# A two-layer transformer kernel: other PSUM banks for three small products, a re-ordered first stretch, and three sums moved behind more products

## The chip, the cores and the metric

The kernel runs on one core of a Trainium2 chip. A core has TensorE (PE; its weight loads are shown as PEld), VectorE (DVE), ScalarE (ACT) and GpSimd (POOL, unused here); SyncE (SP) issues the DMAs, which 16 DMA engines carry out. Each engine works through its own list of instructions in order. The metric is the device time of one execution in microseconds (us).

## The reference, cut to what matters

Two layers over 256 tokens of width 1024. Each is a token mixer with two attentions and a convolutional feed-forward part; every part is modulated by a vector from `c`, and followed by a layer norm.

```python
for l in range(2):
    mod = silu(c) @ w_ada[l] + b_ada[l]            # 6 x 1024
    sh1, sc1, g1, sh2, sc2, g2 = split(mod, 6)
    h = x * (1 + sc1) + sh1
    y = token_mixer(h, ...)
    x = layer_norm(ALPHA * x + g1 * y, ...)
    h = x * (1 + sc2) + sh2
    x = layer_norm(ALPHA * x + g2 * conv_ffn(h, ...), ...)

def token_mixer(h, positions, rel_bias, w_in, ...):
    qa, ka, va, iq, ik, iw, cq, ckv, kr, ga, gb = split(h @ w_in)
    # a: index scores choose 64 of 256 keys per query; softmax(qa.ka + rel_bias[bucket(distance)]) va
    # b: q = rms_norm(cq) @ w_uq, (k, v) = rms_norm(ckv) @ w_ukv, rope on a part; softmax(q.k) v
    merged = sigmoid(ga) * (ya @ w_branch_a) + sigmoid(gb) * (yb @ w_branch_b)
    return merged @ w_out
```

`rel_bias` depends on the position distance through 32 buckets; the kernel builds that table of biases itself, once, from 64 thresholds.

## The kernel before, in words

**Layout.** Activations stand with the 1024 channels as 8 chunks of 128 partitions and the 256 tokens along the free side. Weights come from HBM in one long `stream` of units of up to 128x2048 numbers (1 MB), through four `raw` buffers; a unit's DMA waits until the unit four before it is used up. `advance` walks the stream in order, a few units ahead of use.

**Products in three passes.** `emit_item` splits a unit's 1024 columns into a rounded part `hi` (ACT, line 247) and the rest `lo` (DVE, line 249); activations have the parts `hh` and `hl`. `mm3` (line 298) adds three products of 128x256, so a weight block can be used when ACT and then DVE have converted it. Both have rings of four `hi` and four `lo` buffers.

**Modulation.** Units of kind `ada` aren't multiplied on PE: DVE multiplies such a unit by the broadcast silu(c) (`cb`) and sums along the row (line 231), two sums per unit.

**The first stretch** (layer 0, `layer` with `h0`) goes over 8 chunks `k`: an `ada` unit gives the scale of chunk k (DVE), then `rl` (DVE, line 1054), `hhm` (ACT, line 1055) and `hlm` (DVE, line 1056) give its input, and a unit of `g1` is converted and multiplied into six banks. Three of its twelve column tiles are multiplied in plain f32 (line 472), straight from the raw buffer, which is so held until PE has done that. Into this stretch the code puts the work of the bias table: 8 sign steps per chunk on ACT (`bias_signs`, line 386: 64 in all, tile `step`), blocks of 48 small products on PE (`bias_block`, line 395, tile `bb`, six blocks through the one bank `st`) and their copy on ACT (line 398, `biast`). DVE prepares the thresholds (`bias_prep`) and the rope table (`rope_table`) after chunk 0, and ACT scales x into `XA`.

**Behind it** come the query stage (`main_qa`, tiles `qa..b`), the value stage (`main_va`) with index scores (`side_scores`: tiles `sc`, `rl`, `scr`), the low-rank products (`main_low`: `uq`, `uk`, `uv`), the gates (`main_gate`: `ga`, `gb`) beside the top-64 choice and attention b, then attention a beside `gb` and `wb`. `attention` runs six steps: `logits` (`bl` or `al`), `turn` (transposes `bt` or `at`), `spread` (reciprocal sums `rx`, transposed as `br` or `ar`, copied to `rr`), `values` (`by` or `ay`). `weave` alternates the main generator, which has the large products, with the side one.

**Banks and order.** The eight PSUM banks are `mm` (three), `at` (four) and `st` (one). A scheduler sets each engine's order from the order of the code and its own estimates of time; `tc.issue_after(x)` puts an instruction behind `x` on its engine. Waits follow from data and from buffers becoming free. The layer norm (`ln_begin`) takes an early estimate of the mean from one chunk (`ln10m`, `ln20m`, line 936).

## Time and profile before

| | us |
|---|---|
| median of 3 runs | 810.07 (810.03 to 812.69) |
| profiled execution, whole time | 808.97 |
| its span, first to last instruction | 807.2 |
| PE busy / DVE busy / ACT busy | 779.2 / 684.0 / 522.4 |

The trace is of one execution. The `waits` view lists for how long an engine stood idle and which instruction ended that; the timeline shows instructions in order, with the idle time before them in brackets; the windows view gives busy time, TensorE's granted clock and the DMA share of stretches. A row that says a matmul took 0.28 us shows latency: in a full stream of 128x256 products the next starts 0.11 us later.

### The profile page before, as it was taken

The numbers are of one execution on the slowest core, as the hardware profiler recorded it, in microseconds if no ns is written. First come the engines' busy times: TensorE is split into PE (matmuls) and PEld (weight loads), VectorE is DVE, ScalarE is ACT, GpSimd is POOL, SyncE is SP. The second block draws the span as 40 slices with busy tenths as digits, with TensorE's granted clock in tenths as the row PEclk, the third lists the DMA queues.
The fourth block names the chain that finished last, engine by engine and source line by source line (L and its number), as shares of the span: only waits on it lengthen the run. The fifth ranks groups of instructions, "written<-read, shape, count | busy, mean of one in ns | idle before, by whom it ended". The sixth has DMA issues, their size and how long they took to land.

```text
span 807.2 us, 16613 instructions
## 1 busy us (share of the span) xinstructions
PE 779.2 (97%) x6636; PEld 740.0 (92%) x6636; DVE 684.0 (85%) x1373; ACT 522.4 (65%) x914; POOL 0.2 (0%) x4
## 2 busy tenths in 40 slices
PE   5999999999999999999999999999999999999996
PEld 3898888879999999999999898887999999999995
DVE  6877798999997999899988779967889799897774
ACT  5987566674569766753556756667456976665452
POOL 0000000000000000000000000000000000000000
PEclk9999999999999999999999999999999999999999
DMA  8886747896655575579867665654755555565621
GB/s 303 297 322 230 235 160 283 306 345 242 232 208 168 200 261 194 168 259 338 285 258 287 237 221 174 248 190 180 259 203 181 186 208 198 177 240 196 216 72 53
DMA packets 29727, 182.07 MB, mean 226 GB/s; under 512 B 3857, under 2 KB 5841, under 8 KB 10578
## 3 DMA queue, kind: packets, MB, share of 16 engines
q1 hardware_dynamic: 29650, 181.01, 63.4%
q8 instruction: 52, 0.85, 0.4%
q14 instruction: 25, 0.20, 0.1%
HBM read 178.84 MB, written 1.05 MB: 223 GB/s over the span
## 4 chain that ended last, share of the span: by engine, by line
PE 77%; DVE 11%; ACT 7%; DMA 2%; issue 2%; SPq 0%; ACTq 0%; DVEq 0%
PE dn L298 13%; PE g L298 5%; PE up L298 5%; DVE lo L249 4%; PE va L618 2%; ACT hi L247 2%; DMA raw<-stream 2%; DVE raw L231 1%; PE wo L298 1%; PE uq L298 1%; ACT pr L685 1%; PE ay L723 1%; ACT step L386 1%; PE adap L266 1%; PE by L723 1%
## 5 line engine op out<-in xcount | busy, mean ns | idle before, releaser
L247 ACT ACTIVATE hi<-raw 128x1024 fp32r<-128x1024 f32 (+3 forms) x255 | 254.8, 1004 | 176.4 <-PE dn L298 36.8
L249 DVE TENSOR_TENSOR lo<-raw,hi 128x1024 fp32r<-128x1024 f32 (+3 forms) x255 | 292.6, 1152 | 65.9 <-ACT hi L247 62.5
L231 DVE SCALAR_TENSOR_TENSOR raw<-raw,cb 128x1024 f32<-128x1024 f32 x90 | 107.8, 1218 | 15.0 <-DMA raw<-stream 9.5
L298 PE MATMUL dn<-h2h,hi 128*128 128x256 f32 x352 | 97.5, 277 | 0.0
L298 PE MATMUL dn<-h2h,lo 128*128 128x256 f32 x352 | 97.2, 276 | 0.0
L298 PE MATMUL dn<-h2l,hi 128*128 128x256 f32 x352 | 97.2, 276 | 0.0
L298 PEld LDWEIGHTS dn<-h2l,hi 128*128 128x128 f32 x352 | 66.1, 188 | 0.1
L298 PEld LDWEIGHTS dn<-h2h,hi 128*128 128x128 f32 x352 | 66.1, 188 | 0.1
L298 PEld LDWEIGHTS dn<-h2h,lo 128*128 128x128 f32 x352 | 66.1, 188 | 0.0
L298 PE MATMUL g<-hhm,hi 128*128 128x256 f32 x168 | 45.6, 291 | 5.2 <-ACT hhm L1055 5.2
L298 PE MATMUL g<-hhm,lo 128*128 128x256 f32 x168 | 44.4, 286 | 0.0
L298 PE MATMUL g<-hlm,hi 128*128 128x256 f32 x168 | 42.6, 280 | 0.0
L685 ACT ACTIVATE pr<-pr,mx 128x128 f32<-128x128 f32 x64 | 28.4, 445 | 18.6 <-DVE mx L682 18.6
L298 PEld LDWEIGHTS g<-hhm,hi 128*128 128x128 f32 x168 | 32.0, 195 | 7.3 <-ACT hhm L1055 7.0
L298 PE MATMUL up<-hhf,lo 128*128 128x256 f32 x128 | 34.5, 277 | 0.0
L298 PE MATMUL up<-hhf,hi 128*128 128x256 f32 x128 | 34.4, 281 | 0.1
L298 PE MATMUL up<-hlf,hi 128*128 128x256 f32 x128 | 33.1, 278 | 0.0
L298 PEld LDWEIGHTS g<-hhm,lo 128*128 128x128 f32 x168 | 31.6, 195 | 0.1
L298 PEld LDWEIGHTS g<-hlm,hi 128*128 128x128 f32 x168 | 30.3, 188 | 0.1
L298 PEld LDWEIGHTS up<-hhf,lo 128*128 128x128 f32 x128 | 24.0, 188 | 0.1
L298 PEld LDWEIGHTS up<-hhf,hi 128*128 128x128 f32 x128 | 23.6, 188 | 0.5 <-ACT hhf L1008 0.4
L386 ACT ACTIVATE step<-posf,thr 128x256 bf16<-128x256 f32 (+1 forms) x64 | 23.2, 440 | 1.4 <-DVE thr L354 1.4
(902 smaller groups left out, 2626.3 us busy)
## 6 DMA issues: line engine op xcount, KB each, us to landing
raw<-stream SPq DMA_DIRECT2D x149, 1024.0 KB, 5.1
raw<-stream SPq DMA_DIRECT2D x21, 768.0 KB, 5.8
raw<-stream SPq DMA_DIRECT2D x5, 512.0 KB, 4.3
raw<-stream SPq DMA_DIRECT2D x4, 384.0 KB, 3.8
kT<-rl SPq DMA_DIRECT2D x8, 128.0 KB, 4.5
XB<-xt SPq DMA_DIRECT2D x3, 256.0 KB, 8.0
out<-XA SPq DMA_DIRECT2D x3, 256.0 KB, 2.5
XB<-xt SPq DMA_DIRECT2D x2, 128.0 KB, 6.7
```

What stands on the lines that cost most here:

```text
L231: V.scalar_tensor_tensor(out=raw[:, c:c + D], in0=raw[:, c:c + D], scalar=1.0, in1=cb, op0=OP.mult, op1=OP.mult, accum_out=mod[l][:, j:j + 1])
L247: S.activation(hi[:, a:e], raw[:, c + a:c + e], AF.Copy)
L249: x = V.tensor_sub(lo[:, a:e], raw[:, c + a:c + e], hi[:, a:e].bitcast(F32))
L266: PE.matmul(b[:, :T], ct[:, k:k + 1].to_broadcast([P, P]), raw[:, k * T:(k + 1) * T], start=(k == 0), stop=(k == KD - 1))
L298: state["mm"] = PE.matmul(out, whl[p // 2][:, wcol], xhl[p % 2][xsl], start=start and p == 0, stop=stop and p == 2, skip_group_check=True)
L386: S.activation(st, posf[:, 64 + (0 if g < 32 else P):], AF.Sign, bias=thr[:, g:g + 1])
L618: PE.matmul(b[:, q * T:(q + 1) * T], hx[a][:, k, sl], whl[c][:, kk * T:(kk + 1) * T], start=(k == 0 and q == 0 and n == 0), stop=(k == KD ...
L685: S.activation(p[:, sl], p[:, sl], AF.Exp, bias=mx[:, j:j + 1], scale=-1.0, accum_out=ssum[:, h, j:j + 1])
L723: PE.matmul(yb[0][64 * e:64 * e + 64, c], vals[:, kb, hc], ps[e][:, ps_], start=(kb == 0 and t % 2 == 0), stop=(kb == 1), skip_group_check ...
```

## The change

It has seven parts. **(1)** The start: silu(c) is broadcast by four products of 256 columns from four partitions, in four row strips, instead of two of 512 from one partition. **(2)** The first stretch: 5 sign steps per chunk instead of 8, none in the last chunk, so 35 in the first stretch and 29 behind it; three of the six bias blocks go to the value stage; sign steps, blocks, the bias preparation and the rope table are put behind the work of their chunk (`issue_after`), the rope table behind the last chunk; the scaling into `XA` goes behind the first gate of layer 0. **(3)** In the value stage of layer 0 the rest of the bias work alternates with the scores. **(4)** The mean squares (`rms`) go behind the next `yield` of the main generator. **(5)** `uk` and `uv` use banks `at` instead of `mm`. **(6)** The transposed sums of attention (`br`, `ar`) use a bank `mm` instead of `at`, and stand at the start of the next step. **(7)** The second norm's mean estimate (`ln20m`) stands 24 products later.

```diff
-SIGNS = 8
+SIGNS = 5
...
-    onerow = cp.tile([1, P], F32, name="onerow")
+    onerow = cp.tile([P, P], F32, name="onerow")
-    nc.sync.dma_start(crow, cbc)
+    nc.sync.dma_start(XA[0:97:32, 0], cbc.rearrange("o (a b) -> (o a) b", a=4))
...
-    for h in range(2):
-        b = bank("at", f"cb{h}")
-        PE.matmul(b, onerow, crow[:, h * 512:(h + 1) * 512], start=True, stop=True)
-        S.activation(cb[:, h * 512:(h + 1) * 512], b, AF.Silu)
+    banks = [bank("at", f"cb{i}") for i in range(4)]
+    for i, b in enumerate(banks):
+        PE.matmul(b[:, :T], onerow[32 * i:32 * i + 1], XA[32 * i:32 * i + 1, 0], start=True, stop=True, tile_position=(32 * i, 0))
+    for i, b in enumerate(banks):
+        S.activation(cb[:, i * T:(i + 1) * T], b[:, :T], AF.Silu)
...
-    def rope_table():
+    def rope_table(x):
+        with tc.issue_after(x.ins):
+            V.tensor_scalar_mul(ang, posf[:, 64:], cs[:, C_FRQ:C_FRQ + 1])
...
-        for g in range(KD * SIGNS, 64):
+        for g in range((KD - 1) * SIGNS, 64):
...
+        with tc.issue_after(state["hx"].ins):
+            S.activation(st, posf[:, 64 + (0 if g < 32 else P):], AF.Sign, bias=thr[:, g:g + 1])
...
+                with tc.issue_after(state["mm"].ins):
+                    PE.matmul(b[:, gl * 32:gl * 32 + 32], st, dparts[j], start=(gl == 0 and j == 0), stop=(j == 2),
+                              skip_group_check=True)
...
-            PE.matmul(b[:, :T], ones256, sq[:, 1], start=True, stop=True, skip_group_check=True)
-            PE.matmul(b[:, T:], ones256, sq[:, 0], start=False, stop=True, skip_group_check=True)
...
+            yield
+            b = bank("st", new("rms"))
+            with tc.issue_after(state["mm"].ins):
+                PE.matmul(b[:, :T], ones256, sq[:, 1], start=True, stop=True, skip_group_check=True)
+            PE.matmul(b[:, T:], ones256, sq[:, 0], start=False, stop=True, skip_group_check=True)
...
-                b = bank("mm", new(f"uk{j}"))
+                b = bank("at", new(f"uk{j}"))
...
-                b = bank("mm", new(f"uv{q}"))
+                b = bank("at", new(f"uv{q}"))
...
-                rb = bank("at", new(f"{kind}r{t}"))
+                rr[t] = rx
+
+            def turn_sums(t):
+                rx = rr[t]
+                rb = bank("mm", new(f"{kind}r{t}"))
...
             for step in range(n + 2):
+                if step - 2 in rr:
+                    turn_sums(step - 2)
...
-                    if n == 1 and c == 0 and part == 1:
+                    if n == 1 and c == 1 and part == 0:
                         lnst["after"](0)
...
-        S.activation(XA[:, k], XB[:, k], AF.Copy, scale=ALPHA)
+        with tc.issue_after(state["ga"].ins):
+            S.activation(XA[:, k], XB[:, k], AF.Copy, scale=ALPHA)
```

**Order, place 1: ACT in the first stretch**, from its first sign step (`step`) on; `hhm` is a chunk's input, `hi` its converted weights, `biast` the copy of a bias block. Before:

```order
L386 ACTIVATE step_116<-posf,thr 128x256 x8
L386 ACTIVATE step_117<-posf,thr 128x256 x5
L1055 ACTIVATE hhm_122<-XB,mod_79 128x256
L247 ACTIVATE hi_159<-raw_101 128x1024
L247 ACTIVATE hi_163<-raw_101 128x128
L386 ACTIVATE step_117<-posf,thr 128x256 x3
L386 ACTIVATE step_118<-posf,thr 128x256 x7
L247 ACTIVATE hi_176<-raw_151 128x1024
L247 ACTIVATE hi_249<-raw_151 128x128
L1055 ACTIVATE hhm_122<-XB,mod_79 128x256
L386 ACTIVATE step_118<-posf,thr 128x256
L398 ACTIVATE biast<-bb_366 128x64x8
```

The same place now:

```order
L1075 ACTIVATE hhm_128<-XB,mod_79 128x256
L389 ACTIVATE step_122<-posf,thr 128x256
L246 ACTIVATE hi_165<-raw_107 128x1024
L246 ACTIVATE hi_169<-raw_107 128x128
L389 ACTIVATE step_122<-posf,thr 128x256 x4
L246 ACTIVATE hi_182<-raw_157 128x1024
L246 ACTIVATE hi_252<-raw_157 128x128
L1075 ACTIVATE hhm_128<-XB,mod_79 128x256
L389 ACTIVATE step_122<-posf,thr 128x256 x3
L389 ACTIVATE step_123<-posf,thr 128x256 x2
L1075 ACTIVATE hhm_128<-XB,mod_79 128x256
L389 ACTIVATE step_123<-posf,thr 128x256
```

Thirteen sign steps stood ahead of the second chunk's input and none does now; between the inputs of two chunks stand five instead of eight or more. **DVE at the same place**, from the last piece of chunk 0 to the second chunk's sums (`raw,mod`; `ang` and `kk` are the rope table, `drest`, `dpart` and `dp` the bias preparation). Before, its last rows:

```order
L361 CAST dpart<-drest 128x8
L338 TENSOR_SCALAR kk<-kk 128x256
L363 COPY dp_113<-dpart 32x8 x4
L365 TENSOR_TENSOR drest<-drest,dpart 128x8
L343 SCALAR_TENSOR_TENSOR ang<-kk,ang 128x256
L361 CAST dpart<-drest 128x8
L343 SCALAR_TENSOR_TENSOR ang<-kk,ang 128x256
L231 SCALAR_TENSOR_TENSOR raw_98,mod_79<-raw_98,cb 128x1024 x2
```

Now all that stands there:

```order
L248 TENSOR_TENSOR lo_154<-raw_98,hi_153 128x128
L353 CAST posf<-pos_i 128x320
L354 TENSOR_SCALAR thr<-posf,cs 128x64
L355 TENSOR_SCALAR thr<-thr 128x64
L230 SCALAR_TENSOR_TENSOR raw_104,mod_79<-raw_104,cb 128x1024 x2
```

The second chunk's sums wait for three small instructions instead of for most of the preparation and the table.

**Order, place 2: ACT in the query and value stages of layer 0**, around the first score (`rl<-sc`; `va` is the value copy, `hi` converted weights). Before:

```order
L505 ACTIVATE qa_926<-qa10b_1050 128x512
L247 ACTIVATE hi_1188<-raw_943 128x1024
L562 ACTIVATE rl_1029<-sc_1023 128x384
L562 ACTIVATE rl_1045<-sc_1024 128x384
L398 ACTIVATE biast<-bb_1204 128x64x8
L562 ACTIVATE rl_1075<-sc_1069 128x384
L562 ACTIVATE rl_1091<-sc_1070 128x384
L623 ACTIVATE va_927<-va_1138 128x2x256
```

Now:

```order
L389 ACTIVATE step_127<-posf,thr 128x128 x7
L541 ACTIVATE nh_808<-nf_890 128x768
L389 ACTIVATE step_127<-posf,thr 128x128
L246 ACTIVATE hi_989<-raw_637 128x1024
L389 ACTIVATE step_127<-posf,thr 128x128 x3
L568 ACTIVATE rl_927<-sc_921 128x384
L389 ACTIVATE step_127<-posf,thr 128x128 x5
L568 ACTIVATE rl_955<-sc_922 128x384
L509 ACTIVATE qa_803<-qa10b_936 128x512
L246 ACTIVATE hi_1041<-raw_637 128x1024
L568 ACTIVATE rl_981<-sc_975 128x384
L402 ACTIVATE biast<-bb_1063 128x64x8
```

Sign steps stand among conversions and scores, and three copies of bias blocks follow where there was one.

**Order, place 3: PE in attention b of layer 1**, around the transposed sums `br`. Before:

```order
L694 MATMUL bt_6647<-cs,pr_6572 128x128 x3
L694 MATMUL bt_6653<-cs,pr_6578 128x128 x3
L723 MATMUL by_6669<-cv_6588,vb_5821 64x256
L709 MATMUL br_6662<-cs,rx_6660 128x128 x4
L723 MATMUL by_6669<-cv_6594,vb_5821 64x256
```

Now, 24 gate products (`gb`) later:

```order
L297 MATMUL gb01b_6616<-hhm_5363,hi_6506 128x256
L297 MATMUL gb01b_6616<-hlm_5364,hi_6506 128x256
L297 MATMUL gb01b_6616<-hhm_5363,lo_6507 128x256
L720 MATMUL br_6706<-cs,rx_6666 128x128 x4
L672 MATMUL bl_6713<-kT_5824,qT_5826 128x128
```

The sums no longer stand between the two halves of the values `by`. In layer 1 the mean squares `rms` stand behind the same 29 query products as before; in layer 0 they move from behind 16 to behind 46.

## Rows read from the trace of the kernel before

**Rows 1.** The page, part 1: busy time, share of the span, instructions.

```profile
PE 779.2 (97%) x6636; PEld 740.0 (92%) x6636; DVE 684.0 (85%) x1373; ACT 522.4 (65%) x914; POOL 0.2 (0%) x4
```

**Rows 2.** Waits of PE: who ended them; total us, times, longest.

```profile
PE g L298 <- ACT hhm L1055: 5.2, 1, 5.2
PE uv L604 <- DVE qT L587: 3.1, 2, 1.8
...
PE br L709 <- ACT cv L696: 1.5, 2, 1.1
PE bb L395 <- ACT biast L398: 1.5, 2, 1.1
PE rms L514 <- DVE sq L513: 1.2, 1, 1.2
...
PE ln20m L936 <- DVE XB L912: 0.8, 1, 0.8
...
PE ar L709 <- ACT cv L696: 0.4, 1, 0.4
```

**Rows 3.** Windows: length; busy us of PE, PEld, DVE, ACT, POOL; PEclk, DMA share, GB/s.

```profile
30.00:40.00 10.00, 8.88 (x119) 8.07 (x118) 6.30 (x13) 9.85 (x27) 0.00 (x0) 1.00 0.89 324
...
60.00:70.00 10.00, 9.24 (x62) 7.62 (x61) 7.18 (x10) 9.32 (x13) 0.00 (x0) 1.00 0.93 332
70.00:80.00 10.00, 10.00 (x88) 9.54 (x87) 7.52 (x12) 5.88 (x8) 0.00 (x0) 1.00 0.42 152
80.00:90.00 10.00, 9.05 (x96) 7.11 (x95) 7.16 (x15) 5.06 (x8) 0.00 (x0) 1.00 0.79 195
```

**Rows 4.** Timeline of ACT: start, us, line, operation; idle time before it.

```profile
8.96 0.63 ACT L247 ACTIVATE hi<-raw 128x512 fp32r<-128x512 f32 x1 [0.16 <-DMA raw<-stream]
...
20.56 4.09 ACT L386 ACTIVATE step<-posf,thr 128x256 bf16<-128x256 f32 x10
...
32.57 4.19 ACT L386 ACTIVATE step<-posf,thr 128x128 bf16<-128x128 f32 x14
36.92 1.03 ACT L398 ACTIVATE biast<-bb 128x512 f32<-128x512 f32 x1 [0.15 <-PE bb L395]
...
56.01 1.06 ACT L247 ACTIVATE hi<-raw 128x1024 fp32r<-128x1024 f32 x1 [0.80 <-DMA raw<-stream]
```

**Rows 5.** Timeline of DVE in the first stretch.

```profile
11.97 0.32 DVE L352 CAST posf<-pos_i 128x320 f32<-128x320 int32 x1
...
16.30 1.22 DVE L231 SCALAR_TENSOR_TENSOR raw<-raw,cb 128x1024 f32<-128x1024 f32 x1
...
22.52 1.21 DVE L231 SCALAR_TENSOR_TENSOR raw<-raw,cb 128x1024 f32<-128x1024 f32 x1
...
27.32 1.22 DVE L231 SCALAR_TENSOR_TENSOR raw<-raw,cb 128x1024 f32<-128x1024 f32 x1
...
38.84 1.43 DVE L249 TENSOR_TENSOR lo<-raw,hi 128x1024 fp32r<-128x1024 f32 x2 [1.91 <-ACT hi L247]
...
52.00 1.22 DVE L231 SCALAR_TENSOR_TENSOR raw<-raw,cb 128x1024 f32<-128x1024 f32 x1
```

**Rows 6.** DMA issues from 6.5 to 6.8 us: the second chunk's first unit; us to landing.

```profile
raw<-stream SPq DMA_DIRECT2D x1, 1024.0 KB, 6.5
```

**Rows 7.** Timeline of PE: silu(c) products, the projection's start, what follows it, a bias block.

```profile
2.40 3.75 PE L304 MATMUL cb<-XA,onerow 1*128 1x512 f32 x4 [2.40 <-DMA XA<-cbc]
11.34 0.58 PE L298 MATMUL g<-hhm,hi 128*128 128x256 f32 x1 [5.19 <-ACT hhm L1055]
...
60.98 0.38 PE L522 MATMUL iwt<-cs,misc 128*128 128x128 f32 x2
...
83.31 1.26 PE L395 MATMUL bb<-dp,step 128*128 128x32 bf16 x44
```

**Rows 8.** Windows behind the `uv` of layer 1; columns as in rows 3.

```profile
490.00:491.00 1.00, 1.00 (x7) 1.00 (x6) 1.00 (x6) 0.84 (x2) 0.00 (x0) 0.50 1.00 418
...
489.00:493.00 4.00, 4.00 (x20) 3.76 (x19) 3.98 (x15) 2.50 (x4) 0.00 (x0) 0.57 0.59 238
```

More of the change, by code (lines that the diff above doesn't have):

```diff
@@ L163, in _build @@
     XB = cp.tile([P, KD, T], F32, name="XB")
-    crow = XA[0:1, 0:4].rearrange("p a b -> p (a b)")
-    onerow = cp.tile([1, P], F32, name="onerow")
+    onerow = cp.tile([P, P], F32, name="onerow")
     ct = cp.tile([P, KD], F32, name="ct")
-    nc.sync.dma_start(crow, cbc)
+    nc.sync.dma_start(XA[0:97:32, 0], cbc.rearrange("o (a b) -> (o a) b", a=4))
     V.memset(onerow, 1.0)
@@ L330, in _build @@
     posf = wp.tile([P, 64 + T], F32, name="posf", tag="pr", bufs=5)
-    def rope_table():
+    def rope_table(x):
         ang = wp.tile([P, T], F32, name="ang", tag="pr", bufs=5)
         kk = wp.tile([P, T], F32, name="kk", tag="rsA", bufs=1)
-        V.tensor_scalar_mul(ang, posf[:, 64:], cs[:, C_FRQ:C_FRQ + 1])
+        with tc.issue_after(x.ins):
+            V.tensor_scalar_mul(ang, posf[:, 64:], cs[:, C_FRQ:C_FRQ + 1])
         V.tensor_scalar(kk, ang, 1.0 / (2 * math.pi), cs[:, C_PH + 1:C_PH + 2], OP.mult, OP.add)
@@ L356, in bias_prep @@
         part = cp.tile([P, HEADS], BF, name="dpart")
-        V.tensor_scalar_mul(rest, vec[:, V_R:V_R + 8], 0.5)
+        with tc.issue_after(state["lx"].ins):
+            V.tensor_scalar_mul(rest, vec[:, V_R:V_R + 8], 0.5)
         V.scalar_tensor_tensor(rest, vec[:, V_RP:V_RP + 8], cs[:, C_SG:C_SG + 1], rest, OP.mult, OP.add)
@@ L385, in bias_signs @@
         st = steps[g // 8][:, g % 8] if g < 32 else steps[4 + (g - 32) // 16][:, g % 16]
-        S.activation(st, posf[:, 64 + (0 if g < 32 else P):], AF.Sign, bias=thr[:, g:g + 1])
+        with tc.issue_after(state["hx"].ins):
+            S.activation(st, posf[:, 64 + (0 if g < 32 else P):], AF.Sign, bias=thr[:, g:g + 1])
     def bias_block(n):
@@ L394, in bias_block @@
             for j in range(3):
-                PE.matmul(b[:, gl * 32:gl * 32 + 32], st, dparts[j], start=(gl == 0 and j == 0), stop=(j == 2),
-                          skip_group_check=True)
+                with tc.issue_after(state["mm"].ins):
+                    PE.matmul(b[:, gl * 32:gl * 32 + 32], st, dparts[j], start=(gl == 0 and j == 0), stop=(j == 2),
+                              skip_group_check=True)
         o = (0 if q == 0 else P) + sb * P + half * 64
@@ L479, in layer @@
                     bias_prep()
-                for g in range(k * SIGNS, min(64, (k + 1) * SIGNS)):
+                for g in range(k * SIGNS, (k + 1) * SIGNS if k < KD - 1 else 0):
                     bias_signs(g)
-                if blocks[0] < 6 and (16, 16, 32, 32, 48, 64)[blocks[0]] <= min(64, (k + 1) * SIGNS) - 2:
+                if k < KD - 1 and blocks[0] < 6 and (16, 16, 32, 32, 48, 64)[blocks[0]] <= min(64, (k + 1) * SIGNS) - 2:
                     bias_block(blocks[0])
@@ L490, in layer @@
             S.activation(t[:, o:o + 2].rearrange("p a b -> p (a b)"), banks[j], AF.Copy)
-        S.activation(ik2[64:128], banks[2][0:64, :T], AF.Copy)
+        state["hx"] = S.activation(ik2[64:128], banks[2][0:64, :T], AF.Copy)
         kx = misc[:, 0]
@@ L511, in side_scores @@
             S.activation(sq[:, 0:3], misc[:, 1:4], AF.Square)
-            b = bank("st", new("rms"))
             V.tensor_add(sq[:, 1], sq[:, 1], sq[:, 2])
-            PE.matmul(b[:, :T], ones256, sq[:, 1], start=True, stop=True, skip_group_check=True)
-            PE.matmul(b[:, T:], ones256, sq[:, 0], start=False, stop=True, skip_group_check=True)
             krot = tmp("pr", bufs=5)
@@ L634, in ev @@
                     o = 2 * (i % 2)
-                    S.activation(gt[slot][:, o:o + 2].rearrange("p a b -> p (a b)"), b, AF.Tanh, scale=0.5)
+                    x = S.activation(gt[slot][:, o:o + 2].rearrange("p a b -> p (a b)"), b, AF.Tanh, scale=0.5)
+                    state.setdefault("ga", x)
                 yield from kinner((which, l, i), 2, 4, 2, hx, ev, name=new(f"{which}{i}"))
@@ L748, in chain, with turns @@
                 yield from g
-        weave(chain(main_qa(), main_va()), chain(side_scores(), bias_rest() if l == 0 else iter(())), WV[0], WV[1])
+        def turns(a, b):
+            for _ in a:
+                next(b, None)
+                yield
+            yield from b
+        weave(chain(main_qa(), main_va()), turns(side_scores(), bias_rest() if l == 0 else iter(())), WV[0], WV[1])
         ybhl = (big("iq", new("ybh"), F32R), big("misc", new("ybl"), F32R))
@@ L1053, in h0 @@
         advance(first[("ada", 0, 8 + k, k)] + 1)
-        V.tensor_scalar(hf, XB[:, k], sc, sh, OP.mult, OP.add)
-        S.activation(hh[0][:, k], XB[:, k], AF.Identity, scale=sc, bias=sh)
-        V.tensor_sub(hh[1][:, k], hf, hh[0][:, k].bitcast(F32))
+        x = V.tensor_scalar(hf, XB[:, k], sc, sh, OP.mult, OP.add)
+        state["bar"] = x if k == 0 else None
+        state["hx"] = S.activation(hh[0][:, k], XB[:, k], AF.Identity, scale=sc, bias=sh)
+        x = state["lx"] = V.tensor_sub(hh[1][:, k], hf, hh[0][:, k].bitcast(F32))
         if k == KD - 1:
             consts()
-            rope_table()
+            rope_table(x)
     def xa0(k):
-        S.activation(XA[:, k], XB[:, k], AF.Copy, scale=ALPHA)
+        with tc.issue_after(state["ga"].ins):
+            S.activation(XA[:, k], XB[:, k], AF.Copy, scale=ALPHA)
     nxt, x = h0, xa0
```

## The prediction

> **What bounds the kernel now.** The page's first part comes first: TensorE is busy 779.2 of the span's 807.2 us [rows 1], so nothing here can win much unless TensorE idles less or runs at a higher granted clock; VectorE's and ScalarE's work matters only where TensorE ends up waiting for it. The waits of PE then tell where it idles [rows 2]: 5.2 us once for the first `hhm`, 3.1 us in two waits at `uv`, 1.5 us each at `br` and the bias blocks `bb`, 1.2 us at `rms`, 0.8 us at `ln20m`, 0.4 us at `ar`. The windows add what that list doesn't show, the first stretch: from 30 to 40 us ScalarE is busy 9.85 of 10 us and PE 8.88 [rows 3]. The stretch lasts until `iwt` at 60.98 [rows 7]. Last comes the clock: behind `uv` in layer 1 the granted clock falls to 0.50, which is 1.2 GHz, and over four us it averages 0.57 [rows 8].
>
> All sums are made against the profiled execution, 808.97 us (1.8 us outside its span); the median of the runs shown is 1.1 us above it.
>
> **The first stretch: 6.5 us won, bounds 3.2 and 10.1.** What ScalarE does per chunk: `hi` of 1024 columns 1.06 [rows 4] and a small piece of 128, together 1.15; `hhm`, about half a `hi` of 512 columns and its overhead, 0.5; eight signs at 4.09/10 = 0.41 [rows 4], 3.3; and in some chunks a `biast` of 1.03. That is 4.95 to 6.0, and the pace of the chunks answers it: from the second chunk's sums at 16.30 to the last chunk's at 52.00 are six steps [rows 5], 5.95 us each. VectorE waits for ScalarE (1.91 us at 38.84) [rows 5]. So ScalarE sets the pace. With five signs it has 3.7 to 4.7 a chunk and no longer does.
>
> What is late next is the stream. In the window its share is 0.89 at 5.95 us a chunk [rows 3], so a chunk needs 0.89 × 5.95 = 5.3 us of all queues; I take 5.4, since some gap between two units stays. The bounds are the old pace, 5.95 (something else than the signs holds it), and VectorE's own, 4.8, the one step in which it had nothing to wait for (22.52 to 27.32) [rows 5].
>
> The start moves too. Before, the preparation and most of the rope table stood on VectorE between 11.97 and 16.30 [rows 5], 4.3 us, ahead of the second chunk's sums; 0.6 us of it stays there. Its unit, issued between 6.5 and 6.8, landed after 6.5 us [rows 6], so at 13.1: the sums can start there, not before. The products of silu(c), 3.75 us [rows 7] in two serial pieces, now take four strips at once; that helps only the first `hhm`, which then goes behind the first `hi` at 8.96 (0.63) [rows 4] without thirteen signs near it: the first product comes at about 10.0 instead of 11.34 [rows 7]. This is not added again; the chunks' pace ends the stretch.
>
> Last chunk's sums: 13.1 + 6 × 5.4 = 45.5 against 52.00, won 6.5. At the old pace 13.1 + 35.7 = 48.8, won 3.2; at VectorE's own 13.1 + 28.8 = 41.9, won 10.1. Behind them the stretch ends as before, with the last unit's landing, for which `hi` at 56.01 waited [rows 4].
>
> **Query and value stage of layer 0: 1.6 us lost, bounds 1 won and 4 lost.** Moved in on ScalarE: 29 signs of 128 columns at 4.19/14 = 0.30, 8.7 us, and two `biast` more at 0.95 on average (1.03 in the row), 1.9 [rows 4], together 10.6. ScalarE is busy 9.32 + 5.88 + 5.06 = 20.3 of the 30 us from 60 to 90 [rows 3], so 9.7 are free. Sum against free time: 0.9 too many, but the order alternates them and none may come late for its conversion. PE gains two more blocks: 48/44 × 1.26 = 1.37 [rows 7], 2.7 us; of these the waits at `bb` (1.5 us, [rows 2]) and about 1 us of PE's idle time between 80 and 90 (9.05 busy) [rows 3] take something back. I take 2.7 − 2.0 + 0.9 = 1.6 lost. The end below nothing is that both waits and the idle time go and ScalarE fits (2.7 − 2.5 − 1.2 = 1 won); the other is that nothing hides (2.7 + 0.9) with a half-microsecond stall, 4 lost. The rope table, 2.4 us on VectorE, stands behind the last chunk now, where VectorE is busy 7.18 of 10 [rows 3]: nothing.
>
> **Banks of `uk` and `uv`: 2.8 us won, bounds 1.8 and 3.1.** The products waited for a bank that VectorE had not read out (`qT`), 1.3 us in layer 0 and 1.8 in layer 1, 3.1 in all [rows 2]. With four banks `at` that nobody else needs there, the wait has no cause. I take 1.0 of layer 0, since VectorE is nearly full behind it and hands part back, and all of layer 1.
>
> **The clock behind it: 1.7 us won, bounds 0 and 1.7.** From 489 to 493 the clock averages 0.57 [rows 8], so the work in it would have taken (1 − 0.57) × 4 = 1.7 us less. The fall comes right behind the 1.8 us in which PE stood for `uv` [rows 2]; no such wait, no fall. This is likely, not sure, because it is one execution. The Trainium skill, "TensorE: Matmul & The Clock Gate", section "Part 1: The HAM clock gate (the "warmup" mystery)", describes the gate as watching recent activity by a timing of its own, which would let a fall come at another point or in other runs; by that the term could be nothing. No row before shows a second execution.
>
> **Sums of attention: 1.5 us won, bounds 0.5 and 1.9.** `br` waited 1.1 us in layer 1 and 0.4 in layer 0, `ar` 0.4 [rows 2]: the transposes wanted a bank `at` that ScalarE still had to copy out (`cv`). Now they use a bank `mm`, a step later, with 24 gate products ahead. I keep 1.1 and half of the other 0.8. What it could cost: `rr` comes later for the values behind it, but a whole step lies between. **Mean estimate of the second norm: 0.8 won, bounds 0 and 0.8.** The wait of 0.8 [rows 2] for `XB` is covered by 24 products of 0.11, 2.6 us. **Mean squares: nothing.** In layer 1 `rms` stands behind the same 29 query products as before, so its 1.2 us [rows 2] stay; in layer 0 it is not what waited. `XA`, moved behind the first gate, takes ScalarE's free time: nothing.
>
> Sum: 6.5 − 1.6 + 2.8 + 1.7 + 1.5 + 0.8 = 11.7; 808.97 − 11.7 = 797.3 for the profiled execution, and with the 1.1 us to the median 798.4.
>
> **The rivals.**
>
> *The pace of the first stretch stays.* For it: the share of 0.89 [rows 3] leaves little, and four `raw` buffers each wait for the plain f32 products that come last in their unit. Against it: VectorE's wait ends with ScalarE. It wins 3.2 instead of 6.5: 801.7.
>
> *The clock falls all the same,* here or elsewhere, by a timing that the kernel doesn't set. For it: it is seen once, and its cause is only argued from what stood ahead. 1.7 less: 800.1. The rule of the Trainium skill named above speaks for this one.
>
> *The waits come back at the next instruction.* PE takes `uv` earlier, and then the gates wait for what `uv` waited for; `br` waits in a `mm` bank instead. For it: `qT` is VectorE's work, which doesn't get faster, and VectorE is busy 3.98 of 4 us there [rows 8]. Against it: the gates need VectorE only for converted weights, two units ahead. The terms of banks, clock and sums, 2.8 + 1.7 + 1.5 = 6.0, go: 804.4.
>
> *Slower: ScalarE's order in the query and value stage.* The signs stand in one queue with the conversions, the score copies and the values' copies. If each of them delays a conversion that PE waits for, 10.6 of ScalarE and 2.7 of PE come onto the path, 13.3 instead of 1.6, and a PE that idles so would run for some four us at 0.57 [rows 8], another 1.7: 798.4 + 11.7 + 1.7 = 811.8. It decides from the point where this stage is longer by 13.3 us; against it speaks that ScalarE has 9.7 us free there [rows 3].
>
> *That the change does not do what it says* holds for the mean squares in layer 1 (above, already at nothing).
>
> **How the numbers follow.** Forecast 0.55; old pace 0.17; clock falls 0.09; waits come back 0.10; slower 0.09. The range holds the first four with their bounds: at the lower end the pace goes to VectorE's (3.6 more) and half of the loss in the query stage is spared (2.3 with the end below nothing): 798.4 − 5.9 = 792.5. At the upper end stands the case of returning waits, 804.5. About 0.5%, 4.05 us, is what a measurement of this kernel can tell from no change. Faster than 806.0 are all cases but the slower one, 0.91, less 0.08 for two of them together (old pace and returning waits, 807.7): 0.83. The slower case at 811.8 is within 0.5%; with the old pace, 3.3 more, it goes over 814.1, and I give that half of it and a little, 0.05. The rest, 0.12, is within.
>
> **What would show it right or wrong.** In the changed kernel's profile: the first projection product at about 10 us, the second chunk's sums at about 13, the last chunk's at 45 to 46, and `iwt` at about 54.5; ScalarE clearly under 9 of 10 us in the windows from 30 to 50, and the DMA share above 0.95 instead. From `iwt` to the first `uq` some 1.6 us more than before. No wait at `uv`, no window at 0.50 in layer 1, no wait at `br` and `ln20m`, and the 1.2 us at `rms` still there. Wrong would be the step on the stream if the share stays at 0.89 with ScalarE idle; the step on the query stage, if `iwt` to `uq` grows by more than 5 us; the step on the banks, if `ga` waits in place of `uv`.

## The result

The changed kernel takes 801.74 us (median of 4 runs, 801.0 to 802.03) beside 811.38 for the kernel before on the same chip (810.03 to 814.46). The ratio is 0.9897, with a 95% interval of 0.9868 to 0.9927: 1.0% faster. Timed again on another occasion, it gives 0.9908 (0.9880 to 0.9937). The forecast of 798.4 was 3.3 us too low; the range held the time, and the sign was right. The profiled execution took 802.03 us with a span of 800.3, 6.9 us less than before.

Page, part 1 of the changed kernel, as in [rows 1]:

```profile
PE 772.5 (97%) x6640; PEld 736.6 (92%) x6640; DVE 683.6 (85%) x1373; ACT 521.0 (65%) x916; POOL 0.2 (0%) x4
```

The work is nearly the same, and PE's busy time, in which slow-clock stretches count, fell by 6.7 us. PE's waits, as in [rows 2]:

```profile
PE g L297 <- ACT hhm L1075: 6.6, 1, 6.6
...
PE at L701 <- ACT pr L692: 2.2, 6, 0.8
PE g L476 <- DVE rl L1073: 2.0, 1, 2.0
PE wo01b L297 <- ACT hhg L801: 1.3, 1, 1.3
...
PE rms L529 <- DVE sq L516: 0.8, 2, 0.6
```

`uv`, `br`, `ar`, `bb` and `ln20m` are gone from the list, as intended; of the 1.2 us at `rms`, which were to stay, 0.6 are left here. New are the waits at the transposes `at`, for the probabilities `pr`, and at `wo01b`.

Where the 6.9 us come from is read by setting the first start of a product in the trace of after against that of before. The table does so stage by stage, for the profile taken with the result and for a second profile of the same kernel (run `after_again`, below); plus is won.

| Stage, from the first product of one kind to that of the next | forecast | after | second profile |
|---|---|---|---|
| start to `qa`, layer 0 (first stretch) | +6.5 | +3.6 | +2.4 |
| `qa` to `uq`, layer 0 (query and value stage) | −1.6 | −2.8 | −2.8 |
| `uq` to `ga`, layer 0 (banks) | +1.0 | +1.9 | +1.9 |
| `ga` to `wo`, layer 0 (attention) | +0.4 | −0.6 | −3.6 |
| `wo`, layer 0, to `qa`, layer 1 (norm) | +0.8 | −0.2 | +1.2 |
| `qa` to `uq`, layer 1 (query and value stage) | 0 | +1.8 | +1.2 |
| `uq` to `bl`, layer 1 (banks and clock) | +3.5 | +3.7 | +3.7 |
| `bl` to `wo`, layer 1 (attention) | +1.1 | +1.4 | +1.3 |
| `wo`, layer 1, to the end | 0 | −1.9 | −0.6 |
| sum | +11.7 | +6.9 | +4.6 |

The total came near the rival "the pace stays" (801.7), but not by its account alone: the first stretch won about what that rival says, other terms were too high, and one that I had at nothing won.

**The first stretch.** VectorE in the changed kernel, as in [rows 5]; the rows of line 230 open the sums of chunks 2, 3, 4, 5, 6 and 8:

```profile
13.59 1.23 DVE L230 SCALAR_TENSOR_TENSOR raw<-raw,cb 128x1024 f32<-128x1024 f32 x1 [0.68 <-DMA raw<-stream]
...
21.15 1.22 DVE L230 SCALAR_TENSOR_TENSOR raw<-raw,cb 128x1024 f32<-128x1024 f32 x1
...
26.30 1.22 DVE L230 SCALAR_TENSOR_TENSOR raw<-raw,cb 128x1024 f32<-128x1024 f32 x1
...
30.88 1.43 DVE L248 TENSOR_TENSOR lo<-raw,hi 128x1024 fp32r<-128x1024 f32 x2 [0.93 <-ACT hi L246]
32.23 1.22 DVE L230 SCALAR_TENSOR_TENSOR raw<-raw,cb 128x1024 f32<-128x1024 f32 x1
...
36.90 1.22 DVE L230 SCALAR_TENSOR_TENSOR raw<-raw,cb 128x1024 f32<-128x1024 f32 x1
...
47.22 1.43 DVE L248 TENSOR_TENSOR lo<-raw,hi 128x1024 fp32r<-128x1024 f32 x2 [1.30 <-ACT hi L246]
...
48.90 1.22 DVE L230 SCALAR_TENSOR_TENSOR raw<-raw,cb 128x1024 f32<-128x1024 f32 x1
```

The second chunk's sums start at 13.59, half a microsecond behind the forecast's 13.1, and wait for the unit's landing there, as said. But the step to the third is 7.56 us: the bias preparation stands in it. From the fourth chunk on the steps are 5.93 (26.30 to 32.23), 4.67 (32.23 to 36.90), again 5.93, and 6.07 at the end. The last sums start at 48.90, where the forecast had 45.5 and the old pace 48.8. ScalarE around the fourth chunk shows why a step takes 5.93 (the last row belongs to the last step):

```profile
28.90 0.60 ACT L1075 ACTIVATE hhm<-XB,mod 128x256 fp32r<-128x256 f32 x1 [2.55 <-DVE mod L234]
29.41 0.49 ACT L389 ACTIVATE step<-posf,thr 128x256 bf16<-128x256 f32 x1
29.81 1.24 ACT L246 ACTIVATE hi<-raw 128x1024 fp32r<-128x1024 f32 x2
...
46.12 1.26 ACT L246 ACTIVATE hi<-raw 128x1024 fp32r<-128x1024 f32 x2 [1.87 <-DMA raw<-stream]
```

ScalarE stood idle for 2.55 us at `hhm`, which needs VectorE's sums, and the next unit's conversion `hi` was queued behind it. VectorE then waited for that `hi` (0.93 us, the row at 30.88 above), and its next sums start only after it. The two engines take turns. In the step of 4.67 VectorE waits for nothing. In the last step it waits 1.30 us (the row at 47.22) for a `hi` that had itself waited 1.87 us for its unit: there the stream was late. The windows, as in [rows 3], show that neither ScalarE nor the stream was full:

```profile
30.00:40.00 10.00, 10.00 (x114) 9.55 (x113) 8.89 (x19) 8.12 (x16) 0.00 (x0) 1.00 0.88 334
40.00:50.00 10.00, 9.74 (x108) 8.77 (x107) 7.53 (x14) 8.00 (x17) 0.00 (x0) 1.00 0.82 301
```

The same columns from the second chunk's sums to the last chunk's, first before and then after:

```profile
16.30:52.00 35.70, 32.05 (x377) 29.41 (x376) 29.51 (x68) 34.63 (x85) 0.00 (x0) 1.00 0.82 295
13.59:48.90 35.31, 32.45 (x291) 29.46 (x290) 30.79 (x80) 23.85 (x48) 0.00 (x0) 0.95 0.87 329
```

Before, ScalarE is busy for 34.63 of 35.70 us, so the load of the signs did hold the pace. After, it is busy for 23.85 of 35.31 us, and VectorE, with 30.79 us, is the busier of the two: it has the bias preparation in this stretch now. PE's 10.00 of 10 us from 30 to 40 is no bound of its own: in `a_mix`, below, PE is as busy and the steps are shorter.

Of the other signs named ahead, the first projection product came at 10.57 us (10.0 forecast) and `iwt` at 58.0 (54.5), from where the first `uq` is 2.1 us further off than before (1.6).

**The clock behind `uv` in layer 1**, at 1.00 where [rows 8] had 0.50, and, in the second row, the first stretch, where it now falls, behind PE's wait of 2.0 us for `rl`:

```profile
485.00:489.00 4.00, 4.00 (x38) 4.00 (x37) 4.00 (x14) 3.58 (x5) 0.00 (x0) 1.00 0.59 238
25.00:28.00 3.00, 3.00 (x11) 2.64 (x12) 3.00 (x6) 1.35 (x4) 0.00 (x0) 0.50 1.01 408
```

### The profile page after: what moved, and what is told of

Same layout as the page of the kernel before. It is cut to its first block, busy times and chain, and to the rows that moved or that the text cites. A ratio compares the mean times of both kernels' runs of the same rounds, so it can differ in the third digit from the quotient of the medians.

```text
span 800.3 us, 16631 instructions
## 1 busy us (share of the span) xinstructions
PE 772.5 (97%) x6640; PEld 736.6 (92%) x6640; DVE 683.6 (85%) x1373; ACT 521.0 (65%) x916; POOL 0.2 (0%) x4
## 4 chain that ended last, share of the span: by engine, by line
PE 66%; DVE 17%; DMA 7%; ACT 5%; issue 4%; SPq 0%; ACTq 0%; DVEq 0%
PE dn L297 15%; DMA raw<-stream 7%; PE up L297 6%; DVE lo L248 5%; DVE raw L230 5%; PE va L624 3%; PE g L297 3%; ACT hi L246 2%; PE uq L297 1%; PE wo L297 1%; PE adap L265 1%; DVE scr L651 1%; DVE pr L689 1%; ACT step L389 1%; DVE m L650 1%
```

## The experiments

Every run is set against executions of the kernel before on the same chip, and its ratio is to those. Single executions of one kernel lie up to 1% apart here, and the granted clock goes with that: of 35 executions of the kernel before, the ten shortest (806.2 to 807.3 us) had a mean clock of 0.997 to 0.999, the ten longest (811.3 to 815.1) 0.987 to 0.993.

### Each part alone, in the kernel before

**`e_first`**: parts 1 to 3 of the change.

```diff
-SIGNS = 8
+SIGNS = 5
...
+        with tc.issue_after(state["hx"].ins):
+            S.activation(st, posf[:, 64 + (0 if g < 32 else P):], AF.Sign, bias=thr[:, g:g + 1])
```

> The kernel before with the first three parts of the change alone: the four strips for silu(c), five sign steps a chunk, the bias work put behind the chunks and its rest alternated with the scores. By the prediction: 6.5 us won in the first stretch, 1.6 us given back in the query and value stage, 4.9 us in all. By the trace of the changed kernel, the rival: 3.6 us won up to the first query product, 2.8 us given back before the first uq, so about 1 us faster in all. The last chunk's sums tell it: 45.5 us by the first, about 49 us by the second.

Measured: 0.9976 (0.9954 to 0.9998), 1.9 us won. Its last sums start at 49.12, the first `qa` 3.4 us earlier than before, the first `uq` 0.6 us earlier. The rival's account holds: half the forecast is won in the stretch, and 2.8 us of it go in the query and value stage.

**`e_banks`**:

```diff
-                b = bank("mm", new(f"uk{j}"))
+                b = bank("at", new(f"uk{j}"))
...
-                b = bank("mm", new(f"uv{q}"))
+                b = bank("at", new(f"uv{q}"))
```

> The kernel before with uk and uv in the banks at, and nothing else. By the prediction: no wait at uv, no half clock behind it in layer 1, 4.5 us faster (2.8 for the waits, 1.7 for the clock). The rival: the waits go, but in layer 1 VectorE or the stream hands about 2 us back before the last products of the layer's first half, so 2.5 us faster, with a wait at wo that the kernel before doesn't have.

Measured: 0.9974 (0.9946 to 1.0002), 2.1 us, unclear by its interval. In its trace no PE row names `uv` as waiting, and the stretch from `uq` to `bl` in layer 1 is 3.65 us shorter, the very value of after; 1.0 us is lost again in each layer's attention. The wait at `wo` that the rival expected did not come, but the time is nearer to its 2.5 us than to 4.5. Its profiled execution (812.09 us) spent the time from 87 to 96 us, in the value stage, at half clock, so the time of that one is no measure of the edit.

**`e_sums`**:

```diff
-                rb = bank("at", new(f"{kind}r{t}"))
+                rr[t] = rx
+
+            def turn_sums(t):
+                rx = rr[t]
+                rb = bank("mm", new(f"{kind}r{t}"))
...
+                if step - 2 in rr:
+                    turn_sums(step - 2)
```

> The kernel before with the transposed sums br and ar in a bank mm and a step later, and nothing else. By the prediction: 1.5 us faster, no wait at br or ar. The rival: the waits at br go and others come, at the transposes bt and at for the probabilities pr, and the time stays within 0.7 us.

Measured: 1.0032 (1.0006 to 1.0059), 2.6 us lost, outside both. Three rows of PE's waits in its trace, and the window behind `uv` of layer 1:

```profile
PE uv L604 <- DVE qT L587: 4.4, 2, 3.1
...
PE at L694 <- ACT pr L685: 2.3, 3, 1.5
...
PE wo01b L298 <- ACT hhg L788: 1.3, 1, 1.3
```

```profile
488.00:496.00 8.00, 6.43 (x26) 5.88 (x27) 6.95 (x20) 3.61 (x6) 0.00 (x0) 0.57 0.39 133
```

The waits at `br` and `ar` are gone, with three others in their place. The wait at `uv` in layer 1 grew from 1.8 to 3.1 us although no line of `uv` was touched: the `mm` banks go round in turn, the sums now take some of the turns, and so `uv` may meet an earlier user that is read out later. The half clock behind it lasts longer than in [rows 8]. This part costs time alone, and in the whole change it does not; there `uv` has left these banks. That the turn is the cause is argued from the names, not tried by itself.

**`e_norms`**:

```diff
-                    if n == 1 and c == 0 and part == 1:
+                    if n == 1 and c == 1 and part == 0:
...
+            yield
+            b = bank("st", new("rms"))
+            with tc.issue_after(state["mm"].ins):
+                PE.matmul(b[:, :T], ones256, sq[:, 1], start=True, stop=True, skip_group_check=True)
```

> The kernel before with the mean squares behind the next yield and the second norm's mean estimate 24 products later, and nothing else. By the prediction: 0.8 us faster (the wait at ln20m), the wait at rms in layer 1 stays. The rival, by the trace of the changed kernel, where the stretch from the first query product of layer 1 to uq is 1.8 us shorter: about 2.5 us faster.

Measured: 0.9951 (0.9931 to 0.9970), 4.0 us won, more than both: 1.3 us from `qa` to `uq` in layer 0, 1.7 in layer 1, 1.1 up to the sums of the second norm. The four parts alone sum to 5.4 us.

### Parts taken out of the changed kernel or added to it

**`after_again`**: the changed kernel itself.

> The changed kernel again, beside the three below and on the same chip, so that they can be compared with it. Parts timed alone summed to 5.4 us won (1.9 first stretch, 2.1 banks, 2.6 lost by the sums, 4.0 norms). If the parts add up, it is 5.4 us faster than before; if the parts help each other, as the first result has it, some 8 us.

Measured: 0.9908 (0.9880 to 0.9937), 7.4 us won. The interval reaches from 5.1 to 9.7, so it does not tell 5.4 from 8; what the sums cost alone speaks for parts that help each other.

**`a_nosums`**: the hunk of `e_sums` undone.

```diff
-                rb = bank("mm", new(f"{kind}r{t}"))
+                rb = bank("at", new(f"{kind}r{t}"))
```

> The changed kernel with br and ar back in the banks at and at their old place. By the prediction the sums' part is worth 1.5 us, so this is 1.5 us slower than the changed kernel. The rival, by the waits at the transposes at and at wo that came with it: this is 1 to 2.5 us faster than the changed kernel, the wait of 1.3 us at wo gone.

Measured: 0.9921 (0.9897 to 0.9946), 1.1 us slower than `after_again` by the middle of intervals that overlap. The 1.5 us of the prediction lie within that, the rival's 1 to 2.5 us to the other side do not show. The trace gives both sides. The wait at `br` is back,

```profile
PE br L716 <- ACT cv L703: 1.8, 2, 1.2
```

and the 1.3 us at `wo01b` are gone. From `bl` to the first norm in layer 1 it loses 1.4 us against the kernel before, where the changed kernel's two profiles lose 0.5 and win 0.7; in layer 0 it loses 2.0 us from `ga` to `wo`, within what these two lose (0.6 and 3.6).

**`a_prep`**: the preparation of the bias blocks in three pieces, behind the chunks 2 to 4.

```diff
-        with tc.issue_after(state["lx"].ins):
-            V.tensor_scalar_mul(rest, vec[:, V_R:V_R + 8], 0.5)
...
+        for j in range(3):
+            with tc.issue_after(state["lx"].ins):
...
+            yield
...
-                    bias_prep()
+                    prep = bias_prep()
+                next(prep, None)
```

> The changed kernel with VectorE's bias preparation cut in three, one part behind each of the chunks 2 to 4, instead of some 4 us between the second and the third chunk's sums. If the preparation on VectorE cost what the step from the second to the third sums shows over the others (7.56 us against 5.55 on average), the third sums come at about 19.2 instead of 21.15, PE's wait of 2.0 us for rl and the half clock behind it go, and the first query product comes 2 us earlier. The rival: the stream holds the pace, and the last chunk's sums stay at 48 to 49 us.

Measured: 0.9913 (0.9887 to 0.9939), the same. The third chunk's sums come 1.5 us earlier, as that theory has it, and no half clock is seen there:

```profile
19.66 1.22 DVE L230 SCALAR_TENSOR_TENSOR raw<-raw,cb 128x1024 f32<-128x1024 f32 x1
```

but the last ones start at 49.23: what is won at the third chunk is lost in later steps. So the place of the preparation does not set the end of the stretch. What its work on VectorE costs wherever it stands was not tried.

**`a_nosigns`**: no sign step and no bias block in the first stretch.

```diff
-SIGNS = 5
+SIGNS = 0
```

> The changed kernel with no sign step and no bias block in the first stretch; all 64 and all six follow in the query and value stage. If sign steps on ScalarE held the pace of the first stretch, its last sums come at 45 us or before; if the order of ScalarE's and VectorE's instructions or the stream holds it, they stay at 48 to 49 us. The query and value stage becomes longer by either.

A single execution; its whole time, 829 us, has the 64 signs behind the stretch in it and says nothing. Windows and the last sums:

```profile
30.00:40.00 10.00, 9.30 (x66) 7.84 (x64) 8.98 (x19) 2.89 (x7) 0.00 (x0) 1.00 0.94 357
40.00:50.00 10.00, 7.25 (x45) 5.79 (x45) 6.91 (x14) 2.95 (x6) 0.00 (x0) 1.00 0.96 321
```

```profile
49.52 1.22 DVE L230 SCALAR_TENSOR_TENSOR raw<-raw,cb 128x1024 f32<-128x1024 f32 x1
```

ScalarE is busy under 3 of 10 us and the last sums come no earlier. With five signs a chunk, ScalarE's load is not the bound any more. The end is not the order's alone here: the steps of 5.93 are 5.53, and in the last one, 7.14, VectorE waits 2.37 us for a `hi` whose unit landed late.

**`a_native`**: the three plain f32 tiles of a unit first instead of last.

```diff
-                    [(n, (0, 1, 2)) for n in range(G1)]:
+                    [(n, (0, 1, 2)) for n in (list(range(G1)) if l else [9, 10, 11, 8, 0, 1, 2, 3, 4, 5, 6, 7])]:
```

> The changed kernel with the three plain f32 tiles of a unit multiplied first instead of last, so that a raw buffer comes free when its conversion is done. If the pace of the first stretch is set by the ring (buffer held until PE's last products, then the next unit's landing), the steps between sums fall from 5.9 to about 5.4, as the prediction had it, and the last sums come 2 us earlier. The rival: VectorE and ScalarE as they are ordered, or the queues' bandwidth, hold the pace, and nothing moves by more than 0.5 us.

Measured: 0.9926 (0.9897 to 0.9956), the same. The steps are 5.93, 4.68, 5.93 and 4.68: the last one is shorter (6.07 in the changed kernel), the sums come at 47.63, and the alternation stays. So the pace is something else than the buffers that PE holds. Whether these cost the last step is not shown: `a_nosums` and `a_rms` have the changed kernel's first stretch, instruction for instruction, and their last steps are 4.86 and 6.27, their last sums at 47.91 and 49.20. This run brought an unplanned answer on the clock. Its windows in the value stage, then those of the changed kernel:

```profile
78.00:80.00 2.00, 1.32 (x7) 0.99 (x8) 1.97 (x5) 1.86 (x6) 0.00 (x0) 0.98 0.75 279
80.00:92.00 12.00, 12.00 (x128) 9.37 (x127) 5.35 (x12) 6.01 (x11) 0.00 (x0) 0.50 0.57 166
```

```profile
78.00:80.00 2.00, 1.02 (x5) 0.69 (x6) 1.97 (x4) 1.56 (x6) 0.00 (x0) 1.00 0.91 258
80.00:92.00 12.00, 11.90 (x163) 10.53 (x164) 7.42 (x15) 10.09 (x18) 0.00 (x0) 1.00 0.61 177
```

Ahead of both PE waits 1.1 us once for a score's `rl`. In the one execution the clock then falls to 0.50, 1.2 GHz, for over 12 us, in the other it does not fall. The order of products differs a little between these two; in `a_hi` and `a_mix`, below, it is `a_native`'s from `qa` to `uq`, PE waits 1.1 and 1.0 us at the same place, and the clock stays at 1.00. That stage loses 3.1 us against before in both of them and some 8 in `a_native`, so the fall cost about 5 us.

**`a_hi`**: `a_native`, and ScalarE's conversion of the unit ahead of `hhm` in the fourth and sixth chunk.

```diff
-        state["hx"] = S.activation(hh[0][:, k], XB[:, k], AF.Identity, scale=sc, bias=sh)
+        with after(state["hi", ("g1", 0, k)] if k in (3, 5) else None):
+            state["hx"] = S.activation(hh[0][:, k], XB[:, k], AF.Identity, scale=sc, bias=sh)
```

> The changed kernel with the plain f32 tiles first, as before, and with ScalarE's conversion of a unit put ahead of hhm in the fourth and sixth chunk, where it stood behind. New theory of the pace: in these chunks ScalarE stands 2.55 us at hhm, waiting for VectorE's sums, while a unit that has landed waits behind it; VectorE then waits for that conversion. By it the steps of 5.93 us become about 4.8 (4.67 is what the other chunks take), and the last chunk's sums come at 45 to 46 us instead of 47.6. The rival: the stream holds the pace at 5.3 us a chunk on average, and the last sums stay at 47 to 48.

Measured: 0.9916 (0.9888 to 0.9944), the same in time. The steps from chunk 4 on are 4.93, 6.10, 4.87 and 4.86, the last sums at 47.07. The alternation is gone, and in the step of 6.10 the stream is late: of ScalarE's `hi` the first shown waits 0.23 us for its unit and the second 3.05, and the DMA share is 0.99.

```profile
26.60 1.26 ACT L246 ACTIVATE hi<-raw 128x1024 fp32r<-128x1024 f32 x2 [0.23 <-DMA raw<-stream]
...
34.57 1.25 ACT L246 ACTIVATE hi<-raw 128x1024 fp32r<-128x1024 f32 x2 [3.05 <-DMA raw<-stream]
```

```profile
30.00:40.00 10.00, 9.90 (x112) 9.16 (x111) 8.30 (x19) 6.83 (x14) 0.00 (x0) 1.00 0.99 363
```

**`a_rms`**: the hunk on `rms` of `e_norms` undone.

```diff
-            yield
-            b = bank("st", new("rms"))
```

> The changed kernel with the mean squares back ahead of the yield, so that the scores start twelve query products earlier. By the prediction that part is worth nothing, and this takes the same time as the changed kernel within 0.5 us. By the run with the norms' part alone it is worth up to 3 us, 1.7 of it in layer 1: this is then 1.5 to 3 us slower than the changed kernel, with the stretch from the first query product of layer 1 to uq 30.3 us instead of 28.5.

Measured: 0.9933 (0.9903 to 0.9962), 2.0 us slower than `after_again` (0.9908, on another chip) by the middle of intervals that overlap. From `qa` to `uq` in layer 1 it loses 0.2 us against before, where the changed kernel wins 1.8 and 1.2; PE's wait in that stretch is

```profile
PE rms L518 <- DVE sq L517: 1.4, 1, 1.4
```

and 0.6 and 1.2 us in the changed kernel's two profiles. So the wait alone does not make the stage. The order of the scores does: the first rows are the kernel before, whose order `a_rms` has again, the last two the changed kernel, both at the third group of scores in layer 1.

```profile
463.50 0.48 PE L557 MATMUL sc<-misc,iq 64*128 64x128 f32 x2
464.03 0.37 PE L557 MATMUL sc<-ik,iq 64*128 64x128 f32 x1
...
462.25 0.37 PE L563 MATMUL sc<-misc,iq 64*128 64x128 f32 x1
462.25 0.37 PE L563 MATMUL sc<-ik,iq 64*128 64x128 f32 x1
```

A score uses 64 rows of the array, `misc` one half of them and `ik` the other. Two of different halves start together; where the group opens with two of the same half, the third product starts 0.53 us after the first. The third and fourth group take 1.4 us each before and in `a_rms`, and 0.86 in the changed kernel, 1.1 us in all. The rival's expectation is met in the trace, and in the time by the middle.

**`a_mix`**: `a_hi`, with the sums at their new place in layer 1 alone.

```diff
+                if l == 0:
+                    turn_sums(t, "at")
...
-                if step - 2 in rr:
+                if l and step - 2 in rr:
```

> The changed kernel with the two edits of the first stretch that let the stream set the pace (plain f32 tiles first, ScalarE's conversion ahead of hhm), and the sums br and ar at their new place in layer 1 alone. By the traces the sums at the new place win about 1 us in layer 1 and in layer 0 exchange the wait at br for waits at bt and at; the first stretch wins 1 to 2 us. If these add up: 1.5 to 3 us faster than the changed kernel, 0.987 to 0.989 of before. The rival: what is won ahead of layer 0's attention is given back in it, as in the run with the two edits alone, and this is within 0.3% of the changed kernel.

Measured: 0.9913 (0.9884 to 0.9943), the rival's: the changed kernel's time, not beaten. Its profile was the shortest seen, a span of 799.1. The last sums come at 45.81 us, with the stream full and VectorE nearly so (the last row goes from the second sums to the last):

```profile
30.00:40.00 10.00, 10.00 (x130) 9.58 (x129) 9.14 (x21) 8.03 (x17) 0.00 (x0) 1.00 0.96 372
40.00:50.00 10.00, 10.00 (x117) 9.65 (x114) 9.60 (x23) 8.37 (x19) 0.00 (x0) 1.00 0.99 374
...
13.52:45.81 32.29, 29.28 (x285) 27.06 (x284) 30.60 (x79) 23.78 (x48) 0.00 (x0) 1.00 0.98 375
```

It reaches `qa` 5.6 us earlier than before (the changed kernel 3.6), and `wo` of layer 0 3.4 us earlier (2.1), so of the 2.0 us won in the stretch 1.3 are left there.

## Why the prediction was right or wrong

**The first stretch: the step "What is late next is the stream" failed.** ScalarE's load did set the pace before, as I had it, and with five signs it does so no longer. But the average step went only from 5.95 to 5.89 us: over the last four steps it went from 6.17 to 5.65, and in the first one the preparation now stands. The next bound was the order in which ScalarE and VectorE stand for each other, `hhm` ahead of `hi` in the fourth and sixth chunk. That order stood before the change too (place 1 has it at the second chunk), but its cost could not be seen there: VectorE's wait at 38.84 [rows 5] ended with a `hi` that stood behind fourteen signs and a `biast` [rows 4], which is load. VectorE's wait of 0.92 us for such a `hi` is in all seven profiles with five signs and this order, twice in six of them, and in neither of the two in which the order was changed (`a_hi`, `a_mix`). With that order changed and the f32 tiles first, a step in `a_mix` is 5.38 us on average ((45.81 − 13.52) / 6), where I had 5.4, and the last sums come at 45.81, beside a forecast of 45.5: the stream's share is 0.98 there, and VectorE is busy for 30.60 of 32.29 us, so that these two hold the stretch together. In `a_hi`, with the same first stretch, the average is 5.58. So the stream's step named the second bound and skipped the first. The place of VectorE's preparation was overlooked as well: I took 4.3 us out ahead of the second sums and put them nowhere, and the preparation's part of them stood behind the second sums. So "VectorE's own", 4.8 a chunk, was too low a bound: 30.6 us in six steps are 5.1.

**Query and value stage of layer 0: a term of the right kind and too small.** It lost 2.8 us in `e_first` and in both profiles of after; I took 1.6, with a bound at 4. The slower rival, 13.3 us, was far off.

**Banks and clock: the step was right, what is kept of it was less.** The waits went and nothing came at `ga`. From `uq` to `bl` in layer 1 the 3.5 us forecast were 3.65 in after, in its second profile and in `e_banks`. In layer 0 1.9 were won instead of 1.0, and `e_banks` gives 1.0 back in the attention, where VectorE is nearly full (89 of 95 us busy from 105 to 200 in the kernel before), as I had it. But it gives 1.0 back in layer 1 too, of which I kept all; why is not shown. On the clock the runs allow more than the prediction could: behind `uv` in layer 1 it fell in all four profiles that have the wait there (before, `e_first`, `e_sums`, `e_norms`; 1.8 to 3.1 us) and in none of the ten without it, among them `e_banks`; at `uv` in layer 0 the same four waited 1.3 us, and it did not fall. So this fall belongs to this wait. Two other places behave otherwise. In the value stage of layer 0, with the same order and nearly the same wait ahead, the clock fell in one execution and not in two others (`a_native` against `a_hi` and `a_mix`). In the first stretch it fell in after, its second profile and `a_rms`, and not in `a_nosums`, whose order there is the same, behind a wait of 2.0 us in all four:

```profile
25.00:28.00 3.00, 3.00 (x24) 2.76 (x23) 3.00 (x6) 1.13 (x3) 0.00 (x0) 1.00 1.03 414
```

So the rival "the clock falls all the same, here or elsewhere" is what the profile of after shows, with the fall at another place. That fits what the section of the Trainium skill named in the prediction, "TensorE: Matmul & The Clock Gate", Part 1, says of a gate that watches on a timing of its own. It makes single executions differ by 5 us in one stage, more than most terms of the sum.

**Sums of attention: 1.5 us forecast, 1.1 in the whole change and not clear of noise, 2.6 lost alone.** In layer 1 they win: from `bl` to `wo` after gains 2.8 us on `a_nosums`, of which 1.9 go again behind `wo`. In layer 0 the rival "the waits come back at the next instruction" is what happened: PE waits there for `pr` 1.9 us at `at` and 0.2 at `bt` in after, 2.2 and 2.2 in the second profile, where `a_nosums` has 1.2 and 0.2, and 1.2 at `br`. The wait at `wo01b`, 1.3 us in after, was in no case of mine. In after it is read back to VectorE, which stood at an `ada` unit that had not landed, with the next conversions and `gate` queued behind it:

```profile
562.00 1.22 DVE L248 TENSOR_TENSOR lo<-raw,hi 128x1024 fp32r<-128x1024 f32 x1
565.59 1.22 DVE L230 SCALAR_TENSOR_TENSOR raw<-raw,cb 128x1024 f32<-128x1024 f32 x1 [2.37 <-DMA raw<-stream]
```

It is there in all eight profiles that have the sums at their new place in both layers (0.5 to 1.3 us), and in none that keeps them at the old one in one layer or both. It goes with the landing of that unit: VectorE waits for it 1.2 to 3.4 us in the eight, and 0.7 in `a_mix`, where PE no longer waits. Why the unit lands later with the sums moved is not settled: no run moved them in layer 0 alone.

**Mean estimate of the second norm: right in kind.** The wait went; up to the sums of the norm 1.1 us are won in `e_norms` and in after, 0.8 forecast. In after it is lost again behind them, 0.6 of it in a wait of PE for ScalarE's squares (`ln20q`); the second profile does not have that wait, and its stage wins 1.2.

**Mean squares: "nothing" was wrong.** I looked at where `rms` stands in layer 1, behind the same 29 products, and left it there. But the `yield` ahead of it holds back the scores that follow by twelve query products too, and these are what gains: in all nine profiles with the `yield` there each group of scores opens with products of the two row halves in turn and takes 0.86 us (once 0.99), and in all five without it the third and fourth group open with two of one half and take 1.4 to 1.8. That is 1.1 of the 1.8 us in after; the other 0.6 are PE's shorter wait for `sq`, which the second profile does not have (1.2 us, and 1.2 won). The stage is 1.7 us shorter in `e_norms`, and not at all in `a_rms`. In layer 0 `e_norms` wins 1.3 us; there PE's two waits for a score's `rl`, 0.9 us before, are gone.

**The sum** was right in sign and order of size partly by luck: in the profile 11.7 us were forecast and 6.9 came, and a term at nothing (+1.8) made up for part of what was too high or not foreseen (first stretch, query and value stage, attention and norm of layer 0, and the 1.9 us lost behind `wo` in layer 1). The lower end of the range took 2.3 us from the query stage, where its bounds, from 1.6 lost to 1 won, give 2.6; nothing hangs on that.

## What to carry to other kernels

When an engine's load is lightened, look in the trace at what it waits for and what stands behind that in its queue, before naming a far bound such as the stream: two engines that take turns can hold a pace at which neither is full. Then count the work of the engine that got what was moved. A hunk that moves a `yield` moves all that its generator does afterwards, so the order has to be read for the instructions behind the moved one as well. And a buffer ring is shared: new users of it can change whom the old ones wait for, which is the likely reason that one part cost 2.6 us alone.

## What the runs showed of the hardware

The granted clock fell to half behind one short wait in the value stage in one execution (`a_native`, 1.1 us) and stayed full in two others with the same order and a wait of 1.1 and 1.0 us ahead (`a_hi`, `a_mix`), and having fallen it stayed at 0.50 for 12 us in which PE's busy time was 12.00 of 12.00 (rows of `a_native` above). I had expected a fall to last the 3 to 4 us of [rows 8]. And the order of products that use half of the array's rows has a price: two of different halves start together, and where a group of eight opens with two of the same half it takes 1.4 us or more instead of 0.86.
